# Global average pooling: one input buffer more, sums in place, the last row block in shrinking column chunks, results stored in two parts

## The chip, the cores and the metric

The kernel runs on one core of a Trainium2 chip. The metric is device time in microseconds (us). Every timed comparison with an interval below is between fast runs of a kernel and of the kernel before, which was run beside it; a difference below 2% counts as "the same". Gains of half a percent and less are still read as gains where the interval of the ratio excludes 1. Runs marked "one look" were executed once with a profile and have no interval.

Short names: SP is the queue that issues the DMAs, DVE is VectorE, ACT is ScalarE, PE is TensorE. A *landing* is the moment when a DMA's completion semaphore has its full count.

## The reference

```python
x = np.random.randn(64, 256, 8192).astype(np.float32)
def reference(x):
    return np.mean(x, axis=2)          # out: (64, 256) float32
```

There are 64 x 256 = 16,384 rows of 8192 numbers, 537 MB in all, and one mean a row. The output has 64 KB.

## The kernel before

128 rows lie on the 128 partitions; two such row sets (8.39 MB) are loaded by one DMA. DVE sums one of them, ACT the other. The last two row sets are treated apart to shorten the end: the first is loaded by one DMA and halved between DVE and ACT, the second is loaded in four column quarters through a pool of **two** buffers.

```python
in_pool = ctx.enter_context(tc.tile_pool(name="in", bufs=2))
part_pool = ctx.enter_context(tc.tile_pool(name="part", bufs=2))
...
while t < nbulk:                                   # 126 row sets, two at a time
    xt = in_pool.tile([P, n, S], x.dtype)
    nc.sync.dma_start(out=xt[:], in_=x_v[:, t : t + n, :])
    ...                                            # dve_reduce(row set 0), act_reduce(row set 1)

# row set T-2: one 4 MB load, halves to DVE and ACT
# row set T-1: quarters
for c in range(4):
    xc = part_pool.tile([P, q], x.dtype)
    nc.sync.dma_start(out=xc[:], in_=x_v[:, t2, c * q : (c + 1) * q])
    fn, dst = targets[c]                           # dve, act, dve, act
    fn(dst, xc[:])
...                                                # add the partial sums
# transpose DVE's and ACT's results on PE into one PSUM tile [T, P], scale, store
nc.tensor.matmul(out=resT_ps[:], lhsT=res_d[:], rhs=ident[:], is_transpose=True, start=True, stop=False)
nc.tensor.matmul(out=resT_ps[:], lhsT=res_a[:], rhs=ident[:], is_transpose=True, start=False, stop=True)
nc.vector.tensor_scalar_mul(out=resT[:], in0=resT_ps[:], scalar1=inv)
nc.sync.dma_start(out=outT_v, in_=resT[:])         # 128 runs of 512 B
```

A sum on ACT is an ACTIVATE with `accum_out`; its elementwise result goes to a junk tile of 32 KB a partition.

Of the kernel before, what the change touches and what calls it, by code (L numbers as in the profile page):

```python
# [1 line left out]

# [4 lines left out]

TILES_PER_DMA = 2


@with_exitstack
def kernel(
    ctx: ExitStack,
    tc: tile.TileContext,
    x: bass.AP,
    out: bass.AP,
):
    nc = tc.nc
    P = nc.NUM_PARTITIONS

    B, C, S = x.shape
    N = B * C
    assert N % P == 0, (N, P)
    T = N // P

    x_v = x.rearrange("b c s -> (b c) s").rearrange("(t p) s -> p t s", p=P)
    outT_v = out.rearrange("b c -> (b c)").rearrange("(t p) -> t p", p=P)

    R = TILES_PER_DMA
    assert T >= 2  # L30

    in_pool = ctx.enter_context(tc.tile_pool(name="in", bufs=2))
    part_pool = ctx.enter_context(tc.tile_pool(name="part", bufs=2))
    res_pool = ctx.enter_context(tc.tile_pool(name="res", bufs=1))
    junk_pool = ctx.enter_context(tc.tile_pool(name="junk", bufs=1))
    psum_pool = ctx.enter_context(tc.tile_pool(name="psum", bufs=1, space=bass.MemoryType.PSUM))

    res_d = res_pool.tile([P, T], mybir.dt.float32)
    res_a = res_pool.tile([P, T], mybir.dt.float32)
    nc.gpsimd.memset(res_d[:], 0.0)  # L40
    nc.gpsimd.memset(res_a[:], 0.0)  # L41

    aux_d = res_pool.tile([P, 4], mybir.dt.float32)
    aux_a = res_pool.tile([P, 4], mybir.dt.float32)

    ident = res_pool.tile([P, P], mybir.dt.float32)
    nc.gpsimd.memset(ident[:], 0.0)  # L47
    nc.gpsimd.affine_select(  # L48
        out=ident[:],
        in_=ident[:],  # L50
        compare_op=mybir.AluOpType.not_equal,
        fill=1.0,
        base=0,
        pattern=[[-1, P]],
        channel_multiplier=1,
    )

    inv = 1.0 / float(S)

    def dve_reduce(dst, src):  # L60
        nc.vector.tensor_reduce(  # L61
            out=dst,
            in_=src,
            axis=mybir.AxisListType.X,
            op=mybir.AluOpType.add,
        )

    def act_reduce(dst, src):
        junk = junk_pool.tile([P, src.shape[-1]], mybir.dt.float32)
        nc.scalar.activation(  # L70
            out=junk[:],
            in_=src,
            func=mybir.ActivationFunctionType.Copy,
            accum_out=dst,
        )

    nbulk = T - 2
    t = 0
    while t < nbulk:
        n = min(R, nbulk - t)  # L80
        xt = in_pool.tile([P, n, S], x.dtype)
        nc.sync.dma_start(out=xt[:], in_=x_v[:, t : t + n, :])  # L82
        for j in range(n):
            tt = t + j
            if (tt % 2) == 0:
                dve_reduce(res_d[:, tt : tt + 1], xt[:, j, :])
            else:
                act_reduce(res_a[:, tt : tt + 1], xt[:, j, :])
        t += n

    t1 = T - 2
    half = S // 2
    xt = in_pool.tile([P, S], x.dtype)
    nc.sync.dma_start(out=xt[:], in_=x_v[:, t1, :])  # L94
    dve_reduce(res_d[:, t1 : t1 + 1], xt[:, 0:half])
    act_reduce(res_a[:, t1 : t1 + 1], xt[:, half:S])

    t2 = T - 1
    q = S // 4
    targets = [  # L100
        (dve_reduce, res_d[:, t2 : t2 + 1]),
        (act_reduce, res_a[:, t2 : t2 + 1]),
        (dve_reduce, aux_d[:, 0:1]),
        (act_reduce, aux_a[:, 0:1]),
    ]
    for c in range(4):
        xc = part_pool.tile([P, q], x.dtype)
        nc.sync.dma_start(out=xc[:], in_=x_v[:, t2, c * q : (c + 1) * q])  # L108
        fn, dst = targets[c]
        fn(dst, xc[:])  # L110

    nc.vector.tensor_add(  # L112
        out=res_d[:, t2 : t2 + 1], in0=res_d[:, t2 : t2 + 1], in1=aux_d[:, 0:1]
    )
    nc.scalar.activation(  # L115
        out=res_a[:, t2 : t2 + 1],
        in_=res_a[:, t2 : t2 + 1],
        func=mybir.ActivationFunctionType.Identity,
        bias=aux_a[:, 0:1],
        scale=1.0,  # L120
    )

    resT_ps = psum_pool.tile([T, P], mybir.dt.float32)
    nc.tensor.matmul(  # L124
        out=resT_ps[:], lhsT=res_d[:], rhs=ident[:], is_transpose=True,
        start=True, stop=False,
    )
    nc.tensor.matmul(  # L128
        out=resT_ps[:], lhsT=res_a[:], rhs=ident[:], is_transpose=True,
        start=False, stop=True,  # L130
    )
    resT = res_pool.tile([T, P], mybir.dt.float32)
    nc.vector.tensor_scalar_mul(out=resT[:], in0=resT_ps[:], scalar1=inv)  # L133
    nc.sync.dma_start(out=outT_v, in_=resT[:])


# [1 line left out]
_INS = ['x']  # L138
_OUTS = [((64, 256), 'float32')]


# [23 lines left out]
```

## Time and profile before

| | before |
|---|---|
| median time | 1259.3 us |
| span of the profiled run | 1257.8 us |
| period between landings of 8.39 MB blocks | 19.43 us |
| last bulk block lands | 1227.70 us |
| last load of all lands | 1251.95 us |
| final store issued | 1255.24 us |
| final store landed | 1256.79 us |

Landings are read from the semaphore records of the trace, and the period is the distance of two of them.

First the page of the kernel before. The GB/s row has 40 equal slices of the span; the line of queue 1 gives packets, megabytes, and the share of the 16 DMA engines' time.

```profile
GB/s 402 431 433 434 433 434 434 432 431 426 430 430 434 432 434 433 434 432 431 427 430 430 434 433 432 433 434 432 431 427 431 430 434 431 434 434 433 432 431 259
...
q1 hardware_dynamic: 18000, 536.94, 99.3%
```

The kernel is bound by its load stream. The rate is flat from the second slice to the last but one, and the DMA engines are never idle in between. The Trainium skill, "DMA: Bandwidth & Descriptors", section "Where 436 GB/s comes from", gives a fabric ceiling of 435.2 GB/s; this trace agrees: its 432 GB/s (8.39 MB in 19.43 us) is 1% under it. Only the two ends of the stream leave anything to win, and the last slice, at 259 GB/s, is the one to look into.

Next, what the DMA queue waited for in the last 68 us: who waited, for whom, us in total, times, longest.

```profile
SPq L108 <- DMA xc<-in_x_dram: 22.1, 1, 22.1
...
SPq L108 <- DVE res_d L61: 4.1, 1, 4.1
```

Line 108 issues the quarters. The third and the fourth quarter wait until one of the two chunk buffers has been loaded and summed. The table by stretches shows what that costs; its columns are the stretch, its length, the busy time of each engine with its number of instructions, the PE clock, the busy share of the DMA engines, and GB/s.

```profile
1241.00:1246.00 5.00, 0.00 (x0) 0.00 (x0) 3.56 (x2) 2.72 (x4) 0.00 (x0) 1.00 0.17 38
1246.00:1251.00 5.00, 0.00 (x0) 0.00 (x0) 1.51 (x1) 0.00 (x0) 0.00 (x0) 1.00 0.95 390
```

For 5 us the DMA engines are 17% busy: a bubble in a stream that should have none. Last, the timeline after the last load: start, us, engine, line, operation, and in brackets the idle time before it and what ended it.

```profile
1252.03 1.91 ACT L70 ACTIVATE junk<-xc 128x2048 f32<-128x2048 f32 x1 [7.11 <-DMA xc<-in_x_dram]
...
1254.92 0.29 DVE L133 TENSOR_SCALAR resT<-resT_ps 128x128 f32<-128x128 f32 x1 [2.95 <-PE resT_ps L128]
1255.24 0.35 SPq L134 DMA_DIRECT2D out_dram<-resT  x1
```

From the landing at 1251.95 to the issue of the store at 1255.24, ACT, PE and DVE work one after the other for 3.29 us. The store itself, 128 runs of 512 B, needs this from issue to landing (view of the tile that is stored):

```profile
DMA to landing us min/median/max: 1.5/1.5/1.5
```

### The profile page before, as it was taken

How to read it: one execution, taken by the hardware profiler on the slowest of the kernel's cores; microseconds unless marked ns; L12 is line 12 of the kernel's file. 1: busy time of each engine (PE TensorE's matmuls, PEld its weight loads, DVE VectorE, ACT ScalarE, POOL GpSimd, SP SyncE). 2: the span in 40 equal slices, each digit the busy share in tenths (PEclk: the TensorE clock that was granted, in tenths of full speed). 3: DMA queues.
4: the chain of work that ended last, by engine and by line, in shares of the span. 5: the costliest groups of instructions: out<-in, count | busy, mean ns of one | idle time of the engine just before them, and what ended most of it. 6: DMA issues, size and time to landing. Idle time of an engine off the chain costs nothing.

```text
span 1257.8 us, 460 instructions
## 1 busy us (share of the span) xinstructions
PE 0.9 (0%) x2; PEld 0.4 (0%) x2; DVE 556.6 (44%) x68; ACT 458.0 (36%) x134; POOL 1.0 (0%) x8
## 2 busy tenths in 40 slices
PE   0000000000000000000000000000000000000000
PEld 0000000000000000000000000000000000000000
DVE  2354353453543534435345354353443544535435
ACT  2244243342432423424334243243342433424424
POOL 0000000000000000000000000000000000000000
DMA  9999999999999999999999999999999999999996
GB/s 402 431 433 434 433 434 434 432 431 426 430 430 434 432 434 433 434 432 431 427 430 430 434 433 432 433 434 432 431 427 431 430 434 431 434 434 433 432 431 259
DMA packets 18004, 536.97 MB, mean 427 GB/s; under 512 B 1104, under 2 KB 1232, under 8 KB 1232
## 3 DMA queue, kind: packets, MB, share of 16 engines
q1 hardware_dynamic: 18000, 536.94, 99.3%
q14 instruction: 4, 0.03, 0.0%
HBM read 536.87 MB, written 0.07 MB: 427 GB/s over the span
## 4 chain that ended last, share of the span: by engine, by line
DMA 77%; DVE 22%; issue 0%; ACT 0%; SPq 0%; PE 0%; ACTq 0%
DMA xt<-in_x_dram 77%; DVE res_d L61 22%; DMA xc<-in_x_dram 1%; ACT junk L70 0%; SPq L82 0%; PE resT_ps L128 0%; SPq L108 0%; ACT res_a L115 0%; DVE resT L133 0%; SPq L94 0%; ACTq L70 0%
## 5 line engine op out<-in xcount | busy, mean ns | idle before, releaser
L61 DVE TENSOR_REDUCE res_d<-xt 128x1 f32<-128x8192 f32 x64 | 551.6, 8619 | 690.7 <-DMA xt<-in_x_dram 690.7
L70 ACT ACTIVATE junk<-xt 128x8192 f32<-128x8192 f32 x64 | 446.5, 6976 | 765.3 <-DMA xt<-in_x_dram 765.3
L70 ACT ACTIVATION_READ_ACCUMULATOR junk<-xt 128x1 f32 x64 | 11.9, 186 | 0.0
L70 ACT ACT_TABLE_LOAD x1 | 1.3, 1283 | 22.7 <-DMA xt<-in_x_dram 22.7
L70 ACT ACTIVATE junk<-xc 128x2048 f32<-128x2048 f32 x2 | 3.8, 1910 | 8.3 <-DMA xc<-in_x_dram 8.3
L61 DVE TENSOR_REDUCE aux_d<-xc 128x1 f32<-128x2048 f32 x1 | 2.3, 2286 | 4.9 <-DMA xc<-in_x_dram 4.9
L61 DVE TENSOR_REDUCE res_d<-xc 128x1 f32<-128x2048 f32 x1 | 2.3, 2276 | 0.0
L133 DVE TENSOR_SCALAR resT<-resT_ps 128x128 f32<-128x128 f32 x1 | 0.3, 292 | 3.0 <-PE resT_ps L128 3.0
L124 PE MATMUL resT_ps<-ident,res_d 128*128 128x128 f32 x1 | 0.4, 447 | 1252.1 <-DVE res_d L112 1252.1
L124 PEld LDWEIGHTS resT_ps<-ident,res_d 128*128 128x128 f32 x1 | 0.2, 182 | 1252.1 <-issue 1252.1
L128 PE MATMUL resT_ps<-ident,res_a 128*128 128x128 f32 x1 | 0.5, 472 | 1.8 <-ACT res_a L115 1.8
L70 ACT ACTIVATION_READ_ACCUMULATOR junk<-xc 128x1 f32 x2 | 0.4, 187 | 0.0
L115 ACT ACTIVATE res_a<-res_a,aux_a 128x1 f32<-128x1 f32 x1 | 0.3, 295 | 0.0
L48 POOL TENSOR_SCALAR_AFFINE_SELECT ident<-ident 128x128 f32<-128x128 f32 x1 | 0.3, 292 | 0.1
L40 POOL MEMSET res_d<- 128x128 f32 x1 | 0.2, 204 | 0.3 <-POOLq L149 0.3
L41 POOL MEMSET res_a<- 128x128 f32 x1 | 0.2, 204 | 0.0
L47 POOL MEMSET ident<- 128x128 f32 x1 | 0.2, 204 | 0.0
L128 PEld LDWEIGHTS resT_ps<-ident,res_a 128*128 128x128 f32 x1 | 0.2, 183 | 2.1 <-ACT res_a L115 2.1
L112 DVE TENSOR_TENSOR res_d<-res_d,aux_d 128x1 f32<-128x1 f32 x1 | 0.2, 159 | 0.0
L149 POOL MEMSET const-bfloat16-1.0<- 128x1 bf16 x1 | 0.1, 101 | 0.0
L149 POOL MEMSET const-uint8-127<- 128x1 uint8 x1 | 0.1, 101 | 0.0
L149 POOL MEMSET const-float32-0.0<- 128x1 f32 x1 | 0.1, 98 | 0.2 <-issue 0.2
(1 smaller groups left out, 0.1 us busy)
## 6 DMA issues: line engine op xcount, KB each, us to landing
xt<-in_x_dram SPq DMA_DIRECT2D x63, 8192.0 KB, 30.1
xt<-in_x_dram SPq DMA_DIRECT2D x1, 4096.0 KB, 20.9
xc<-in_x_dram SPq DMA_DIRECT2D x4, 1024.0 KB, 15.0
out_dram<-resT SPq DMA_DIRECT2D x1, 64.0 KB, 1.5
```

The costliest lines, as they stand in the source:

```text
L40: nc.gpsimd.memset(res_d[:], 0.0)
L41: nc.gpsimd.memset(res_a[:], 0.0)
L47: nc.gpsimd.memset(ident[:], 0.0)
L48: nc.gpsimd.affine_select(out=ident[:], in_=ident[:], compare_op=mybir.AluOpType.not_equal, fill=1.0, base=0, pattern=[[-1, P]], channel_m ...
L61: nc.vector.tensor_reduce(out=dst, in_=src, axis=mybir.AxisListType.X, op=mybir.AluOpType.add,)
L70: nc.scalar.activation(out=junk[:], in_=src, func=mybir.ActivationFunctionType.Copy, accum_out=dst,)
L112: nc.vector.tensor_add(out=res_d[:, t2 : t2 + 1], in0=res_d[:, t2 : t2 + 1], in1=aux_d[:, 0:1])
L115: nc.scalar.activation(out=res_a[:, t2 : t2 + 1], in_=res_a[:, t2 : t2 + 1], func=mybir.ActivationFunctionType.Identity, bias=aux_a[:, 0:1 ...
L124: nc.tensor.matmul(out=resT_ps[:], lhsT=res_d[:], rhs=ident[:], is_transpose=True, start=True, stop=False,)
L128: nc.tensor.matmul(out=resT_ps[:], lhsT=res_a[:], rhs=ident[:], is_transpose=True, start=False, stop=True,)
L133: nc.vector.tensor_scalar_mul(out=resT[:], in0=resT_ps[:], scalar1=inv)
L149: nc = _bacc.Bacc("TRN2", target_bir_lowering=False, num_devices=1)
```

## The change

The intent is to keep the load queue full to the very end, and to leave as little work as possible after the last byte. The main lines of the diff, shortened where it says `...` (`P` = 128, `R` = 2, `LB` = index of the last 8.39 MB block):

```diff
+BULK_BUFS = 3
+LAST_CHUNKS = (4096, 2048, 1024, 512, 512)
...
+    out_bulk = o_v[0 : LB * P * R].rearrange("(n r p) -> n r p", p=P, r=R)
+    out_last = o_v[LB * P * R : N].rearrange("(r p) -> p r", r=R)
...
-    in_pool = ctx.enter_context(tc.tile_pool(name="in", bufs=2))
+    in_pool = ctx.enter_context(tc.tile_pool(name="in", bufs=BULK_BUFS))
...
-        nc.scalar.activation(out=junk[:], in_=src, func=Copy, accum_out=dst)
+        nc.scalar.activation(out=src, in_=src, func=COPY, accum_out=dst)
...
+    xl = in_pool.tile([P, R, S], x.dtype, name="xt")     # the whole last block has one buffer
+    nc.sync.dma_start(out=xl[:, 0, :], in_=x_v[LB, :, 0, :])
+    ...                                                  # halves to DVE and ACT
+    for c, w in enumerate(LAST_CHUNKS[:-1]):
+        ld = nc.sync.dma_start(out=xl[:, 1, pos : pos + w], in_=x_v[LB, :, 1, pos : pos + w])
+        ...                                              # halves to DVE and ACT, sums into fin_in
+    with tc.issue_after(ld.ins):
+        nc.sync.dma_start(out=fin_in[:, 0:lastw], in_=x_v[LB, :, 1, pos:S])
...
+    # first 126 row sets: transposed by PE and stored early, as 63 packets of 1 KB in the trace
+    nc.sync.dma_start(out=out_bulk, in_=bulk[:LB])
+    # last chunk and the partial sums beside it: scaled and summed by one DVE instruction
+    nc.vector.tensor_scalar(out=fin_in[...], in0=fin_in[...], scalar1=inv, ..., accum_out=fin[:, 1:2])
+    nc.sync.dma_start(out=out_last, in_=fin[:])          # [128, 2]: 256 writes of 4 B
```

The last store skips the transpose: each partition writes its two results, 4 B each, straight to the output.

More of the change, by code (lines that the diff above doesn't have):

```diff
@@ L6 @@
 from concourse._compat import with_exitstack
-TILES_PER_DMA = 2
+ROWS = 2
+BULK_BUFS = 3
+LAST_CHUNKS = (4096, 2048, 1024, 512, 512)
 @with_exitstack
@@ L19 @@
     P = nc.NUM_PARTITIONS
+    F32 = mybir.dt.float32
+    X = mybir.AxisListType.X
+    ADD = mybir.AluOpType.add
+    COPY = mybir.ActivationFunctionType.Copy
     B, C, S = x.shape
     N = B * C
-    assert N % P == 0, (N, P)
-    T = N // P
-    x_v = x.rearrange("b c s -> (b c) s").rearrange("(t p) s -> p t s", p=P)
-    outT_v = out.rearrange("b c -> (b c)").rearrange("(t p) -> t p", p=P)
-    R = TILES_PER_DMA
-    assert T >= 2
-    in_pool = ctx.enter_context(tc.tile_pool(name="in", bufs=2))
-    part_pool = ctx.enter_context(tc.tile_pool(name="part", bufs=2))
-    res_pool = ctx.enter_context(tc.tile_pool(name="res", bufs=1))
-    junk_pool = ctx.enter_context(tc.tile_pool(name="junk", bufs=1))
-    psum_pool = ctx.enter_context(tc.tile_pool(name="psum", bufs=1, space=bass.MemoryType.PSUM))
-    res_d = res_pool.tile([P, T], mybir.dt.float32)
-    res_a = res_pool.tile([P, T], mybir.dt.float32)
-    nc.gpsimd.memset(res_d[:], 0.0)
-    nc.gpsimd.memset(res_a[:], 0.0)
-    aux_d = res_pool.tile([P, 4], mybir.dt.float32)
-    aux_a = res_pool.tile([P, 4], mybir.dt.float32)
-    ident = res_pool.tile([P, P], mybir.dt.float32)
+    R = ROWS
+    assert R == 2 and N % (P * R) == 0, (N, P, R)
+    NB = N // (P * R)
+    LB = NB - 1
+    assert 1 <= LB <= P and sum(LAST_CHUNKS) == S
+    inv = 1.0 / float(S)
+    x_v = x.rearrange("b c s -> (b c) s").rearrange("(n r p) s -> n p r s", p=P, r=R)
+    o_v = out.rearrange("b c -> (b c)")
+    out_bulk = o_v[0 : LB * P * R].rearrange("(n r p) -> n r p", p=P, r=R)
+    out_last = o_v[LB * P * R : N].rearrange("(r p) -> p r", r=R)
+    in_pool = ctx.enter_context(tc.tile_pool(name="in", bufs=BULK_BUFS))
+    res_pool = ctx.enter_context(tc.tile_pool(name="res", bufs=1))
+    psum_pool = ctx.enter_context(
+        tc.tile_pool(name="psum", bufs=1, space=bass.MemoryType.PSUM)
+    )
+    res = [res_pool.tile([P, NB], F32, name=f"res{r}") for r in range(R)]
+    ident = res_pool.tile([P, P], F32)
     nc.gpsimd.memset(ident[:], 0.0)
@@ L56 @@
     )
-    inv = 1.0 / float(S)
-    def dve_reduce(dst, src):
-        nc.vector.tensor_reduce(
-            out=dst,
-            in_=src,
-            axis=mybir.AxisListType.X,
-            op=mybir.AluOpType.add,
-        )
-    def act_reduce(dst, src):
-        junk = junk_pool.tile([P, src.shape[-1]], mybir.dt.float32)
-        nc.scalar.activation(
-            out=junk[:],
-            in_=src,
-            func=mybir.ActivationFunctionType.Copy,
-            accum_out=dst,
-        )
@@ L77 @@
-    nbulk = T - 2
-    t = 0
-    while t < nbulk:
-        n = min(R, nbulk - t)
-        xt = in_pool.tile([P, n, S], x.dtype)
-        nc.sync.dma_start(out=xt[:], in_=x_v[:, t : t + n, :])
-        for j in range(n):
-            tt = t + j
-            if (tt % 2) == 0:
-                dve_reduce(res_d[:, tt : tt + 1], xt[:, j, :])
-            else:
-                act_reduce(res_a[:, tt : tt + 1], xt[:, j, :])
-        t += n
-    t1 = T - 2
-    half = S // 2
-    xt = in_pool.tile([P, S], x.dtype)
@@ L94 @@
-    nc.sync.dma_start(out=xt[:], in_=x_v[:, t1, :])
-    dve_reduce(res_d[:, t1 : t1 + 1], xt[:, 0:half])
-    act_reduce(res_a[:, t1 : t1 + 1], xt[:, half:S])
-    t2 = T - 1
-    q = S // 4
-    targets = [
-        (dve_reduce, res_d[:, t2 : t2 + 1]),
-        (act_reduce, res_a[:, t2 : t2 + 1]),
-        (dve_reduce, aux_d[:, 0:1]),
-        (act_reduce, aux_a[:, 0:1]),
-    ]
-    for c in range(4):
-        xc = part_pool.tile([P, q], x.dtype)
-        nc.sync.dma_start(out=xc[:], in_=x_v[:, t2, c * q : (c + 1) * q])
-        fn, dst = targets[c]
-        fn(dst, xc[:])
@@ L112 @@
-    nc.vector.tensor_add(
-        out=res_d[:, t2 : t2 + 1], in0=res_d[:, t2 : t2 + 1], in1=aux_d[:, 0:1]
-    )
-    nc.scalar.activation(
-        out=res_a[:, t2 : t2 + 1],
-        in_=res_a[:, t2 : t2 + 1],
-        func=mybir.ActivationFunctionType.Identity,
-        bias=aux_a[:, 0:1],
-        scale=1.0,
-    )
-    resT_ps = psum_pool.tile([T, P], mybir.dt.float32)
-    nc.tensor.matmul(
-        out=resT_ps[:], lhsT=res_d[:], rhs=ident[:], is_transpose=True,
-        start=True, stop=False,
-    )
@@ L128, with dve_sum, act_sum @@
-    nc.tensor.matmul(
-        out=resT_ps[:], lhsT=res_a[:], rhs=ident[:], is_transpose=True,
-        start=False, stop=True,
-    )
-    resT = res_pool.tile([T, P], mybir.dt.float32)
-    nc.vector.tensor_scalar_mul(out=resT[:], in0=resT_ps[:], scalar1=inv)
-    nc.sync.dma_start(out=outT_v, in_=resT[:])
+    def dve_sum(dst, src):
+        nc.vector.tensor_reduce(out=dst, in_=src, axis=X, op=ADD)
+    def act_sum(dst, src):
+        nc.scalar.activation(out=src, in_=src, func=COPY, accum_out=dst)
@@ new lines @@
+    for n in range(LB):
+        xt = in_pool.tile([P, R, S], x.dtype, name="xt")
+        nc.sync.dma_start(out=xt[:], in_=x_v[n])
+        dve_sum(res[0][:, n : n + 1], xt[:, 0, :])
+        act_sum(res[1][:, n : n + 1], xt[:, 1, :])
+    nparts = 2 * len(LAST_CHUNKS)
+    lastw = LAST_CHUNKS[-1]
+    xl = in_pool.tile([P, R, S], x.dtype, name="xt")
+    fin_in = res_pool.tile([P, lastw + nparts], F32)
+    fin = res_pool.tile([P, R], F32)
+    head = res_pool.tile([P, 2], F32)
+    half = S // 2
@@ new lines @@
+    nc.sync.dma_start(out=xl[:, 0, :], in_=x_v[LB, :, 0, :])
+    dve_sum(head[:, 0:1], xl[:, 0, 0:half])
+    act_sum(head[:, 1:2], xl[:, 0, half:S])
+    pos, k = 0, 0
+    for c, w in enumerate(LAST_CHUNKS[:-1]):
+        ld = nc.sync.dma_start(
+            out=xl[:, 1, pos : pos + w], in_=x_v[LB, :, 1, pos : pos + w]
+        )
+        mid = pos + w // 2
+        dve_sum(fin_in[:, lastw + k : lastw + k + 1], xl[:, 1, pos:mid])
+        act_sum(fin_in[:, lastw + k + 1 : lastw + k + 2], xl[:, 1, mid : pos + w])
+        k += 2
+        pos += w
@@ new lines @@
+    with tc.issue_after(ld.ins):
+        nc.sync.dma_start(out=fin_in[:, 0:lastw], in_=x_v[LB, :, 1, pos:S])
+    nc.vector.tensor_scalar(
+        out=head[:],
+        in0=head[:],
+        scalar1=inv,
+        scalar2=None,
+        op0=mybir.AluOpType.mult,
+        op1=ADD,
+        accum_out=fin[:, 0:1],
+    )
+    bulk = res_pool.tile([P, R, P], F32)
+    for r in range(R):
+        ps = psum_pool.tile([P, P], F32, name=f"ps{r}")
+        nc.tensor.transpose(out=ps[:LB, :], in_=res[r][:, 0:LB], identity=ident[:])
+        nc.vector.tensor_scalar_mul(out=bulk[:LB, r, :], in0=ps[:LB, :], scalar1=inv)
@@ L138 @@
+    nc.sync.dma_start(out=out_bulk, in_=bulk[:LB])
+    nc.vector.tensor_scalar(
+        out=fin_in[:, 0 : lastw + k],
+        in0=fin_in[:, 0 : lastw + k],
+        scalar1=inv,
+        scalar2=None,
+        op0=mybir.AluOpType.mult,
+        op1=ADD,
+        accum_out=fin[:, 1:2],
+    )
+    nc.sync.dma_start(out=out_last, in_=fin[:])
 _INS = ['x']
```

## The prediction

> **What bounds the kernel now.** The load stream. The page's DMA row is 9 in 39 of 40 slices, queue 1 is busy 99.3%, and the GB/s row reads 431 to 434. By landings, one 8.39 MB block takes 19.43 us (432 GB/s). The Trainium skill, "DMA: Bandwidth & Descriptors", section "Where 436 GB/s comes from", gives 435.2 GB/s as the fabric ceiling; the trace agrees, lying 1% under it. DVE (8.69 us a block) and ACT (7.03 us) idle over half of each period, always for the load (groups by line: 691 and 765 us of idle time). The DVE share in the chain of waits (22%) is misleading: the DMA engines stay busy meanwhile, because the other buffer's load is already queued.
>
> So only the ends can be shortened:
> 1. Head: first landing at 22.6 us. Unchanged.
> 2. A bubble in the tail. The timeline shows the last bulk block landing at 1227.7, the 4 MB row at 1237.9, quarter chunks at 1240.4 and 1242.8. Chunk 3 is issued only when a chunk buffer is free: the queue's waits show 22.1 us for it, and the DMA packets show nearly no traffic from 1241 to 1246.5. The last chunk lands at 1251.95 instead of about 1247: about 4.5 to 5 us lost.
> 3. After the last byte: ACT 1.91 + 0.19 + 0.29, PE 0.5, DVE 0.29, output issue at 1255.24, landing 1256.8, end 1257.8. That is 5.8 us.
>
> **What the change does.**
> - Third bulk buffer: the queue is never empty already, so 0 us in the steady state. It lets all loads of the last block be queued around 1198 to 1200, once block 60 is reduced.
> - In-place ACT output instead of a junk tile: 0 us; same size of ACTIVATE (7.03 us), half of it idle anyway.
> - The last block has no buffer reuse: bubble gone. Packets of 32 KB take 1218 ns and of 8 KB 309 ns, so about 6 ns fixed each; row 0 plus the five chunks (16, 8, 4, 2, 2 KB packets, 8 an engine) are estimated at 19.8 us. An instruction fetch of 8 KB delayed one engine 0.5 us in this stretch before; it may again. Last landing about 1247.7 (saves 4.2).
> - After the last byte: one DVE tensor_scalar over 520 columns, estimated 0.72 us (reduce slope 1.04 ns a column plus fixed), instead of 3.2 us of ACT, PE and DVE (saves about 2.5). ACT's last small pieces (256 columns, estimated 0.41 + 0.19) end around 1247.8, about when the last chunk lands. Two PE transposes, two scalings and the bulk store (63 x 2 rows of 512 B) are hidden behind loads or beside the last sum.
> - The final store becomes 256 writes of 4 bytes. The same page ("Specifications") says under 512 B the DMA does read-modify-write; no run shows its cost yet. I add 0.3 us to the 1.55 us from issue to landing.
>
> Sum: 1247.85 + 0.72 + 0.1 + 1.85 + 1.0 = 1251.5 us span, against 1257.8; the timed figure was 1.5 us above the span, so **1253.0 us**, range 1251.3 to 1255.0. Faster by over 2%: 1%; within 2%: 98%; slower: 1%.
>
> **What would show it.** Period between landings still 19.43 us; GB/s still 431 to 434; no DMA gap after 1241; last load landing 1247 to 1248.3; DVE's final TENSOR_SCALAR about 0.7 us starting within 0.3 us of that landing; output landing 1.6 to 2.2 us after issue. Longest waits of the DMA queue still on DVE, though harmless.
>
> **What would make it wrong.** A steady period that shifts with three loads queued (0.1 us a block is 6 us); small packets slower than 6 ns fixed each; 4-byte writes costing over 1 us; the bulk store (63 rows, perhaps on fewer DMA engines) delaying the final store; instruction fetches hitting the slowest engine.

## The result, and the profile after

| | before | after |
|---|---|---|
| median time, 4 runs each | 1259.30 us | 1259.97 us |
| span of the profiled run | 1257.8 us | 1258.3 us |
| period between landings of blocks | 19.43 us | 19.43 us |
| last bulk block lands | 1227.70 us | 1228.08 us |
| last load lands | 1251.95 us | 1247.76 us |
| final store issued | 1255.24 us | 1248.63 us |
| final store landed | 1256.79 us | 1257.37 us |

The ratio is 1.0005, with a 95% interval of 0.9991 to 1.0019: the same. A ratio here is taken over the fast runs of both kernels, so it need not be quite the ratio of the medians quoted.

The page after, to be held against the one of before:

```profile
GB/s 401 432 433 433 433 433 433 432 429 433 428 429 431 434 433 433 432 433 432 430 431 430 428 433 433 433 433 431 433 432 430 431 430 429 432 433 433 433 431 255
...
q1 hardware_dynamic: 18344, 536.94, 99.2%
```

The stream is as it was, and the last slice is no fuller (255 GB/s against 259). That row alone would suggest that nothing happened in the tail. The stretches say otherwise:

```profile
1241.00:1246.00 5.00, 0.00 (x0) 0.00 (x0) 4.48 (x5) 3.41 (x5) 0.00 (x0) 1.00 0.99 398
1246.00:1251.00 5.00, 0.00 (x0) 0.00 (x0) 2.20 (x5) 1.51 (x6) 0.00 (x0) 1.00 0.11 30
```

The bubble is gone (busy share 0.99 instead of 0.17), and the loads are over 4.2 us earlier. The timeline of the changed kernel's end:

```profile
1247.90 0.69 DVE L114 TENSOR_SCALAR_CACHE_REDUCE fin_in<-fin_in 128x520 f32<-128x520 f32 x1 [0.35 <-DMA fin_in<-in_x_dram]
1248.52 0.08 DVE L114 DVE_READ_ACCUMULATOR fin_in<-fin_in 128x1 f32 x1
1248.63 0.41 SPq L123 DMA_DIRECT2D out_dram<-fin  x1
```

The store is issued 6.6 us sooner than before, as intended. And then nothing is left to do but wait. The queue's waits, and the view of the stored tile:

```profile
SPq L149 <- DMA out_dram<-fin: 8.1, 1, 8.1
```

```profile
DMA to landing us min/median/max: 8.7/8.7/8.7
```

The final store of 1 KB takes 8.7 us from issue to landing, where the 64 KB store of before took 1.5. The sum closes: the last load 4.19 us sooner, the work between it and the store 2.42 us shorter (0.87 instead of 3.29), the store 7.19 us longer (8.74 instead of 1.55), the stretch after it 0.1 us shorter, together +0.5 us, which is the difference of the two spans.

The packet records of the changed kernel show where in the store the time passes. The last of its packets starts at 1249.79, but the 16 counts of its semaphore arrive singly between 1254.68 and 1257.37. So the engines had started every packet within 1.2 us of the issue, and the confirmations came late. The Trainium skill, "DMA: Bandwidth & Descriptors", section "Anatomy of one DMA — SWDGE (gpsimd) path", says of the fixed cost of a DMA that it is mostly completion latency: the semaphore can't count until the last byte is confirmed in the target memory. It says this of DMAs issued by GpSimd; this one is issued by SP. This trace agrees with that order of events (packets sent first, counts up to 7.6 us later), though the page's account of about 2 us is far from this 8.7.

### The profile page after: what moved, and what is told of

Its sections match the earlier page's. It is cut to its first block, busy times and chain, and to the rows that moved or that the text cites. A ratio compares the mean times of both kernels' runs of the same rounds, so it can differ in the third digit from the quotient of the medians.

```text
span 1258.3 us, 464 instructions
## 1 busy us (share of the span) xinstructions
PE 0.9 (0%) x2; PEld 0.4 (0%) x2; DVE 557.5 (44%) x74; ACT 458.0 (36%) x137; POOL 0.7 (0%) x6
## 4 chain that ended last, share of the span: by engine, by line
DMA 82%; DVE 15%; another core or an unknown queue 2%; SPq 0%; issue 0%; DVEq 0%
DMA xt<-in_x_dram 78%; DVE res L61 15%; DMA fin_in<-in_x_dram 4%; SPq L86 0%; SPq L68 0%; DVE fin_in L114 0%; SPq L80 0%; DVEq L114 0%; DVEq L149 0%
## 5 line engine op out<-in xcount | busy, mean ns | idle before, releaser
L61 DVE TENSOR_REDUCE res<-xt 128x1 f32<-128x8192 f32 x63 | 547.2, 8686 | 689.6 <-DMA xt<-in_x_dram 689.6
L64 ACT ACTIVATE xt<-xt 128x8192 f32<-128x8192 f32 (+2 forms) x68 | 450.5, 6625 | 788.9 <-DMA xt<-in_x_dram 788.8
L64 ACT ACTIVATION_READ_ACCUMULATOR xt<-xt 128x1 f32 x68 | 12.7, 186 | 0.0
L61 DVE TENSOR_REDUCE fin_in<-xt 128x1 f32<-128x2048 f32 (+3 forms) x4 | 4.6, 1153 | 0.4 <-DMA xt<-in_x_dram 0.4
L61 DVE TENSOR_REDUCE head<-xt 128x1 f32<-128x4096 f32 x1 | 4.4, 4420 | 0.2 <-DMA xt<-in_x_dram 0.2
```

The costliest lines, as they stand in the source:

```text
L61: nc.vector.tensor_reduce(out=dst, in_=src, axis=X, op=ADD)
L64: nc.scalar.activation(out=src, in_=src, func=COPY, accum_out=dst)
```

## The experiments

Eleven kernels were run. The theory to test: **256 writes of 4 B next to each other are slow to be confirmed, because of their form.** Rivals: the final store is slow for where it stands (it follows the bulk store and the end of a 537 MB stream), or any small write has a cost of its own wherever it goes.

### 1. The same kernel with a store of long runs (`row_store`)

```diff
-    nc.sync.dma_start(out=out_last, in_=fin[:])
+    nc.tensor.transpose(out=ps_fin[:], in_=fin[:], identity=ident[:])     # [128, 2] -> [2, 128]
+    nc.vector.tensor_copy(out=fin_row[:], in_=ps_fin[:])
+    nc.sync.dma_start(out=out_last_rows, in_=fin_row[:])                  # 2 runs of 512 B
```

> The changed kernel, but the last block's 256 results are transposed by PE and stored as two runs of 512 B in place of 256 writes of 4 B. Theory (the small writes cost the 8.7 us from issue to landing): issue to landing falls to 1.5 to 2 us as in the kernel before, PE and DVE add about 0.9 us, time about 1254 us (6 us under the changed kernel). Rival (the final store is slow because it follows the bulk store or the end of the load stream, whatever its form): landing stays near 8.7 us, time 1260 to 1261.

Measured: correct, 1253.12 us against 1259.15 for before, ratio 0.9952 (0.9935 to 0.9968). Its timeline:

```profile
1248.91 0.37 PE L124 MATMUL ps_fin<-ident,fin 128*2 128x128 f32 x1 [11.63 <-DVE fin_in L114]
1249.32 0.28 DVE L126 COPY fin_row<-ps_fin 2x128 f32<-2x128 f32 x1 [0.47 <-PE ps_fin L124]
1249.63 0.26 SPq L127 DMA_DIRECT2D out_dram<-fin_row  x1
```

And what the queue waited for after it had issued the store, where the changed kernel had 8.1 us:

```profile
SPq L153 <- DMA out_dram<-fin_row: 0.6, 1, 0.6
```

PE and DVE move the issue 0.75 us further from the final sum (0.78 us from the end of DVE's accumulator read at 1248.85 to the issue at 1249.63, where the changed kernel had 0.03), and the store lands at 1250.74 (semaphore records), 1.1 us after its issue instead of 8.7. The added work and the landing are both a little shorter than expected (0.9 us, and 1.5 to 2 us). The same data at the same place in the program, after the same bulk store, is fast when it is written in long runs. The rival of place falls. The changed kernel's own trace agrees: its bulk store landed at 1248.04 (semaphore records), before the final store was issued at 1248.63.

### 2. Only the bubble removed from the kernel before (`before_part4`)

```diff
-    part_pool = ctx.enter_context(tc.tile_pool(name="part", bufs=2))
+    part_pool = ctx.enter_context(tc.tile_pool(name="part", bufs=4))
```

> The kernel before with four chunk buffers instead of two, nothing else. If the bubble in the load stream costs what I read from the packets, the last load lands about 1247 instead of 1251.95 and the time falls by 4.5 to 5 us, to about 1254.5. Rival (the bubble is filled by something else, or the queue would stall anyway): no gain, 1259.

Measured: correct, 1255.24 us against 1259.15, ratio 0.9969 (0.9954 to 0.9984); the last load lands at 1247.61. In the stretches:

```profile
1241.00:1246.00 5.00, 0.00 (x0) 0.00 (x0) 4.16 (x3) 2.49 (x4) 0.00 (x0) 1.00 0.98 408
```

One digit in the old kernel gives 3.9 us, a little less than expected, since the last load lands 4.3 us sooner (between the two profiled runs, which are of different sittings) rather than 4.5 to 5. So the bubble was what the packets said, and it was caused by the reuse of two chunk buffers.

### 3. Neither a third buffer nor in-place sums (`row_store_plain`)

```diff
-BULK_BUFS = 3
+BULK_BUFS = 2
...
-        nc.scalar.activation(out=src, in_=src, func=COPY, accum_out=dst)
+        junk = junk_pool.tile([P, S], F32, name="junk")
+        nc.scalar.activation(out=junk[:, 0 : src.shape[-1]], in_=src, func=COPY, accum_out=dst)
```

(Edits to the kernel of experiment 1.)

> The version with the last block stored as two 512 B runs, but with two input buffers instead of three and a separate junk tile for ACT's output instead of in-place. My theory: neither a third buffer nor in-place output is worth anything, since the load queue was never empty between blocks; time 1253.1 us within 0.4, landing period 19.43 us. Rival (the third buffer is part of what closes the tail bubble, or in-place writing costs or saves): 1254 us and more, or a visible gap between loads.

Measured: correct, 1253.09 us against 1259.40 on its chip, ratio 0.995 (0.9934 to 0.9967), period 19.43 us. The third buffer and the in-place output, the two most visible parts of the change, are together worth nothing that these runs can see. With two buffers the loads of the last block are issued between 1217.0 and 1219.3 us instead of 1198.0 and 1200.3 as in the changed kernel, and both are early enough: the queue still holds the last bulk block until 1227.7. (They were undone together. That each is worth nothing alone, and not a gain and a loss that cancel, was not shown.)

### 4. What is slow about the small writes

All runs here keep the changed kernel up to the final store and change only where its writes of 4 B go. Except for `pair_8B` the result is wrong. All but that one are one look each; what is read from them is the time from issue to landing. How well a landing repeats was not measured by itself; the four timed runs of the changed kernel lie within 0.34 us, those of `pair_8B` within 0.46 us. So differences of 1 us and more are read, and smaller ones are not.

```python
# spread_256: step of 256 B;  step8_pr: step of 8 B (s=2)
spread = o_v[0 : 2*P*s].rearrange("(p r s) -> p r s", r=R, s=s)[:, :, 0:1]      # s=64
# step8_rp: step of 8 B (s=2);  step16_rp: step of 16 B (s=4)
spread = o_v[0 : 2*P*s].rearrange("(r p s) -> p r s", r=R, s=s)[:, :, 0:1]
nc.sync.dma_start(out=spread, in_=fin[:].rearrange("p (r o) -> p r o", o=1))
# half_count: one of the two columns only, 128 writes in 512 contiguous bytes
nc.sync.dma_start(out=out_last[:, 1:2], in_=fin[:, 1:2])
# group64: 128 writes in 8 groups of 64 B, 512 B apart (a=8, b=16);  group32: 16 groups of 32 B (a=16, b=8)
grp = o_v[0 : a*128].rearrange("(a s) -> a s", s=128)[:, 0:b]
nc.sync.dma_start(out=grp, in_=fin[:, 1:2])
# pair_8B: the last block's rows dealt so that partition p has rows 2p and 2p+1 (correct result)
x_p = x.rearrange("b c s -> (b c) s").rearrange("(n p r) s -> n p r s", p=P, r=R)
out_last = o_v[LB*P*R : N].rearrange("(p r) -> p r", r=R)                       # 128 writes of 8 B
```

> The changed kernel with the 256 final writes of 4 B kept, but each to its own 256 B of the output (result wrong on purpose). Theory A (writes of 4 B that fall into the same stretch of HBM wait for each other): issue to landing falls to 1.5 to 2.5 us, span about 1252. Theory B (each write under 512 B costs by itself, wherever it goes): landing stays near 8.7 us, span 1258.

> The changed kernel storing only one of the last two rows: 128 writes of 4 B, contiguous 512 B in all (half of the last block's results missing on purpose). Theories A and B: the part of the landing above the 1.5 us floor halves, landing 4.5 to 5.5 us, span about 1254.5. Rival (a fixed cost of any store under 512 B or of any read-modify-write): landing stays 8.7 us.

> The changed kernel's 256 writes of 4 B, each 8 B from the next (wrong result on purpose), so that half as many fall into each stretch of the output, in the same order over partitions as in the changed kernel. Theory A (writes to one small granule wait for each other, granules go in parallel): the excess over the 1.9 us of the spread run halves from 6.8 us, issue to landing about 5.3 us. Rival (any two writes in one larger stretch, or close in time, cost the whole): 8 us and more. If landing is already at 2 us, the granule is 8 B or less.

> The same with a step of 16 B. Theory A: the excess is a quarter, issue to landing about 3.6 us. Rival: 8 us and more.

> A step of 8 B again, but with a partition's two results next to each other, so that by the order of partitions each 64 B stretch gets its 8 writes from four neighbouring partitions instead of eight. Theory A as it stands (only the count per stretch matters): as with the other run of 8 B step, about 5.3 us. Rival (the conflict is between different DMA engines writing one stretch, which four neighbouring partitions would not bring about): about 2 us.

> The run with 128 writes of 4 B, but in 8 groups of 64 contiguous bytes (16 writes each) that lie 512 B apart (wrong result on purpose). If the conflict is inside a stretch of 64 B or less, nothing is relieved: issue to landing near the 7.7 us of the contiguous 512 B. Rival (the conflict is over a stretch of 128 B to 512 B, which now holds 16 writes instead of 32 to 128, fewer than the 32 that cost nothing with a step of 16 B): about 1.6 to 2 us.

> The same in 16 groups of 32 contiguous bytes (8 writes each), 512 B apart. If the stretch that counts is 32 B or less, landing again near 7.7 us; if it is 64 B, the count per stretch is that of the step of 8 B, landing about 2.8 us; if larger, 1.6 to 2 us.

> The changed kernel with the last block's rows dealt so that each partition holds two neighbouring rows: the final store is then 128 writes of 8 B over the same 1 KB, with a correct result. If the count of writes per stretch decides, this is like a step of 8 B: issue to landing 2.5 to 3.5 us, time about 1254.2 us. Rival (any partial write into a contiguous stretch costs as before): landing over 7 us, time about 1259.

Measured (issue to landing; "per 512 B" counts the writes that fall into 512 B of the output, worked out from the layout; the landing of `group64` is read from the semaphore records):

| run | writes | laid out | per 512 B | issue to landing, us |
|---|---|---|---|---|
| changed kernel | 256 of 4 B | contiguous, 1 KB | 128 | 8.7 |
| half_count | 128 of 4 B | contiguous, 512 B | 128 | 7.7 |
| pair_8B | 128 of 8 B | contiguous, 1 KB | 64 | 3.0 |
| step8_pr | 256 of 4 B | step 8 B | 64 | 3.4 |
| step8_rp | 256 of 4 B | step 8 B | 64 | 2.8 |
| step16_rp | 256 of 4 B | step 16 B | 32 | 1.6 |
| group64 | 128 of 4 B | 64 B in each 512 B | 16 | 1.9 |
| group32 | 128 of 4 B | 32 B in each 512 B | 8 | 1.9 |
| spread_256 | 256 of 4 B | step 256 B | 2 | 1.9 |

The lines of five of them, each the view of the stored tile: `half_count`, `step8_rp`, `step16_rp`, `group32`, `pair_8B`.

```profile
L123 SPq DMA_DIRECT2D out_dram<-fin x1: 370/370/370, 1248.5 to 1248.5; - x1
...
DMA to landing us min/median/max: 7.7/7.7/7.7
```

```profile
L124 SPq DMA_DIRECT2D out_dram<-fin x1: 410/410/410, 1248.5 to 1248.5; - x1
...
DMA to landing us min/median/max: 2.8/2.8/2.8
```

```profile
L124 SPq DMA_DIRECT2D out_dram<-fin x1: 410/410/410, 1248.7 to 1248.7; - x1
...
DMA to landing us min/median/max: 1.6/1.6/1.6
```

```profile
L124 SPq DMA_DIRECT2D out_dram<-fin x1: 665/665/665, 1248.5 to 1248.5; - x1
...
DMA to landing us min/median/max: 1.9/1.9/1.9
```

```profile
L124 SPq DMA_DIRECT2D out_dram<-fin x1: 365/365/365, 1248.7 to 1248.7; - x1
...
DMA to landing us min/median/max: 3.0/3.0/3.0
```

What follows:

- **It is neither the size nor the number of the writes by itself.** With a step of 16 B, the same 256 writes of 4 B land in 1.6 us (3.6 expected), as fast as the old store of 512 B runs. A cost of each small write by itself falls.
- **It is how densely they lie, and more steeply than I had thought.** Twice the distance brings the 8.7 us to 2.8, not to the 5.3 that I had expected from a cost in proportion to the writes per stretch; four times the distance takes the rest. Half the writes at the same density (`half_count`) stay at 7.7 us, where I had expected 4.5 to 5.5.
- **The stretch seems to be longer than 64 B; this is argued, not shown.** 16 contiguous writes in 64 B landed in 1.9 us when the rest of their 512 B was left alone (`group64`), while `half_count`, which fills the 512 B, took 7.7 us. Had any 16 writes within 64 B been enough for the conflict, `group64` would have been slow. But the two group runs change more than this: only 16 or 8 partitions write into any one 512 B, where 128 do in `half_count`, and `group64` also ran on fewer DMA engines, as its landing counts show (9 separate increments instead of 16), though `group32` did not. That fewer writers in one stretch made them fast is not excluded. All runs with at most 32 writes per 512 B were fast, those with 64 took 2.8 to 3.4 us, those with 128 took 7.7 and more; whether the stretch is 128, 256 or 512 B these runs do not separate.
- **It is not only a matter of who writes into a stretch.** In `step8_pr` and `step16_rp` partition p writes at byte 16p; its second write goes to byte 16p + 8 in the one and to 16p + 2048 in the other. So the same partitions share each stretch of up to 2 KB in both, and `step8_pr` has twice as many writes in it. It took 3.4 us against 1.6. Placing neighbouring partitions' writes together did not help either: 3.4 us against the 2.8 of `step8_rp`. Of that difference 0.23 us is a longer issue (0.64 against 0.41 us in the trace), which `spread_256` has too; the rest is too small to be read from one look each.
- **The place in the output moved too, and does not explain the table.** The spread, step and group runs write from the start of the output, which the bulk store has just written; the changed kernel, `half_count`, `pair_8B` and `row_store` write into its last 1 KB. With 64 writes per 512 B both places gave about the same (3.0 us at the end, 2.8 and 3.4 us at the start). Contiguous writes of 4 B at the start were not run.
- `pair_8B`, a correct kernel, took 1254.12 us against 1259.37 (ratio 0.9958, 0.9942 to 0.9975), as expected from its count per stretch.

The Trainium skill, "DMA: Bandwidth & Descriptors", section "Specifications", says that under 512 B a DMA does read-modify-write. That many such operations on one stretch of memory wait for each other would fit the table, but no run shows the inside of the memory; it stays an argument.

## Why the prediction was wrong

The time is 1259.97 us; the forecast was 1253.0, range 1251.3 to 1255.0. It stayed within 2%, as forecast, but 5 us above the top of the range. Point by point:

- **Load stream bounds, third buffer and in-place sums worth nothing in the steady state: right.** The period stayed at 19.43 us, and experiment 3 undid both parts without effect. (The GB/s row, though, never read "431 to 434" throughout: between its ends it has 426 to 434 before and 428 to 434 after.)
- **Bubble gone, last landing about 1247.7: right**, 1247.76. That it is so close is in part luck: the last bulk block landed 0.38 us later than before, and the last block then took 19.68 us, where the estimate was 19.8 and perhaps 0.5 more for a fetch. Experiment 2 shows the same from the other side.
- **Small load packets with about 6 ns fixed each: near enough.** In the trace the 2 KB packets took 87 ns against 82 by that estimate.
- **One DVE instruction of about 0.72 us after the last byte, store issued near 1248.67: right**, 0.69 plus 0.08 us for the accumulator read, issue at 1248.63.
- **1.0 us after the store's landing: right**, 0.89.
- **Final store, "I add 0.3 us to the 1.55 us from issue to landing": wrong.** It took 8.74 us. This is the one term of the sum that was mis-sized, by 6.9 us (8.74 for 1.85), and the miss of the whole (7.0 us) is nearly all that term. I had listed "4-byte writes costing over 1 us" among the dangers, but kept it out of the range.

How the step failed: the text names the read-modify-write and adds 0.3 us, as if the form of the store were a small extra; how densely the writes lie does not enter, and nothing measured stands behind the 0.3. No run of this case had shown a single write under 512 B to the output; the only measured store was of 128 runs of 512 B. The runs show that such writes can be nearly free (1.6 us in all for 256 of them) or ruinous (8.7 us), by how densely they lie. The contiguous layout of 4 B writes, which looks the friendliest, is the worst of those tried. So the path after the store's issue, taken as nearly fixed, was the longest piece of the tail.

The gain was therefore earned in full, the final store being issued 6.6 us sooner, and spent in the landing of that store. The version that keeps it (experiment 1, 1253.12 us) beats the kernel before by half a percent in runs made side by side, and lies 6.9 us under the changed kernel's 1259.97, which was not run beside it; with two buffers and the junk tile it does as well.

## What to carry to other kernels

At the end of a kernel like this one the store's landing is on the critical path, all of it, so cost its layout as carefully as the loads: a transpose on PE and a copy on DVE cost 0.75 us here, and the store in runs of 512 B that they allow landed 7.6 us sooner after its issue than the column writes of 4 B. In this stream, which already kept the DMA engines 99% busy, a third bulk buffer (with in-place sums) brought nothing that could be seen, while two more chunk buffers in the tail brought 3.9 us. So look for the places where the queue runs dry, here a pool of two chunk buffers in the tail, and read them from the DMA share by stretches, not from the averages of the page. When a plan has one term that no trace has measured, give the range that term's uncertainty, not that of the measured ones.

## What the Trainium skill lacked or had wrong

- "DMA: Bandwidth & Descriptors", sections "Specifications" and "Rules for kernel authors": they warn of transfers under 512 B and under 64 KB, but not that the time depends on how densely small writes to HBM lie. Here 256 writes of 4 B, contiguous, took 8.7 us from issue to landing, with a step of 8 B 2.8 to 3.4 us, with a step of 16 B 1.6 us.
- The same page, section "Anatomy of one DMA — SWDGE (gpsimd) path", puts the fixed cost at about 2 us (measured there on the GpSimd path) and has no such figure from issue to landing for a store that SP issues. Here a store of 2 runs of 512 B landed 1.1 us after its issue, one of 128 runs of 512 B 1.55 us, and the 256 contiguous writes of 4 B 8.7 us.
- The same page, section "Where 436 GB/s comes from", says that for HBM to SBUF the HBM side (about 358 GB/s) binds, while "HBM Reference", section "Specifications (TRN2)", has a core that streams alone well above that. This kernel, on one core, read at 432 GB/s, so here the second holds.
- "Runtime: NRT & Kernel Launch", section "Instruction fetch mechanics", calls the cost of crossing from one block of instructions to the next mostly hidden. It lacks what such a fetch can do to a load stream (the profile lists the fetches as queue 14). In the kernel before, the fetch of 8 KB that starts at 395.9 us falls into a block period of 19.91 instead of 19.43 us, and the distance between the first and the last engine's count of a block goes from 0.50 to 0.97 us and does not come back; in the changed kernel the fetch at 881.8 us falls into a period of 20.12 us. Not every fetch shows: the one at 754.1 us in the kernel before left the period as it was. The cause is read from the order of time, and no run tested it.
